# A two-layer decoder trunk in fp32: the lower part of every fourth weight chunk is formed on GpSimd instead of VectorE

## The chip, the cores and the metric

The kernel runs on one core of a Trainium2 chip. The metric is device time in microseconds (us) of one execution, as the median of a few runs. A profiler recorded one execution; its times are used for everything below that is finer than the whole run. Five engines work side by side and meet through semaphores: TensorE (PE, its weight loads shown as PEld), VectorE (DVE), ScalarE (ACT), GpSimd (POOL) and SyncE (SP, which here issues nearly all DMAs).

## What is computed

Two layers, each on 256 rows of width 2048. In short (`S`, `sigmoid` and `rms` as usual, everything fp32):

```python
h = rms_norm(x, norm_g[l])
proj = h @ w_in[l]                      # 2048 x 18496, split into the parts of four branches
y_pool = pool_mixer(pv, pool_w, pool_scale) * silu(pz)      # causal means over 2, 4, 8, 16 rows
y_mla  = mla_mixer(cq, ckv, kr, ...) * silu(mz)             # 8-head latent attention with rotary part
y_conv = conv_mixer(cb, cc, cx, conv_w) * silu(cz)          # gated convolution of width 3
y_mem  = memory_xattn(xq, rms_norm(mem) @ w_mem_kv, ...) * silu(xz)
merged = sum(sigmoid(gpre[i] + gate_b[i]) * (y[i] @ w_branch[l, i]) for i in range(4))
x = x + merged @ w_out[l]
```

Nearly all arithmetic is in the products with the weights, which are read once each: 478 MB in all.

## The kernel before

**A product in three terms.** TensorE multiplies operands in a reduced-precision fp32 form (type fp32r). To get close to fp32, every operand is kept as two fp32r tiles: `hi`, the value rounded by a copy into that type, and `lo`, what is left, `value - hi`. A product is then hi·hi + hi·lo + lo·hi. The activations' pairs are made once and kept; the weights' pairs are made as the weights arrive.

**Chunks.** The weights lie packed in HBM in the order of use, in chunks of 128 partitions by up to 1024 elements (512 KB); there are 884 of them in the two layers. The generator `wchunks` (L293) handles a chunk in three steps: L303 loads it into `raw` (issued by SP), L304 rounds it into `hi` on ACT, L305 subtracts, `lo = raw - hi`, on DVE. All three stand under `tc.high_priority(AHEAD)`, with AHEAD = 100, so that the framework's scheduler places them ahead of other work that comes earlier in the program. There are four `raw` buffers, three `hi` and three `lo`, used in turn: the chunk that comes three later can write its `hi` only after TensorE has finished with the present one.

**Consumers.** `tm_block` (L308 on) uses a chunk as the moving operand: per chunk twelve matmuls of 128x512, in threes L317 (activation hi, weight hi), L318 (activation hi, weight lo) and L319 (activation lo, weight hi). `fm_block` uses it as the stationary operand: per chunk eight pairs L323 (weight hi, 512 columns) and L324 (weight lo, 256 columns). Every block accumulates in one of three PSUM tiles `acc`; the layer's other work (transposes at L350, L401, L459 and others, attention, norms, gates) runs beside the blocks, with its TensorE parts between the blocks' matmuls.

**What sets the order.** A scheduler of the framework orders each engine's instructions at build time, by its own estimate of when each would be ready; an engine then works strictly in that order. POOL holds almost nothing before: some constants and twelve small fills, of `pv` at L738 and of `u` at L783.

**The start.** The first four blocks (chunks 1 to 32) are the keys and values of the memory. Beside them the kernel takes the statistics of x: four row loads at L386, each followed by two squares with a sum on ACT (L197, `junk`), then a chain of small DVE operations (L376, then L185 to L191) that ends in `rx` (L377). Two transposes at L401 spread `rx` over the partitions, and the operands of `h` are made from it.

Of the kernel before, what the change touches and what calls it, by code (L numbers as in the profile page):

```python
# [10 lines left out]
F32 = mybir.dt.float32  # L11
# [3 lines left out]
ALU = mybir.AluOpType  # L15
# [95 lines left out]
def tile_hybrid_trunk(  # L111
    ctx: ExitStack, tc: tile.TileContext, x, xT, mem, memT, positions, vectors, mla_g, gate_b, weights, consts, out,
):
    nc = tc.nc
    V, A, T = nc.vector, nc.scalar, nc.tensor
# [12 lines left out]
    def nm(s):  # L128
        uid[0] += 1
        return f"{s}{uid[0]}"  # L130
# [147 lines left out]
    def step():  # L278
        if background:
            run = background.pop(0)  # L280
            if run is not None:
                run()
# [5 lines left out]
    def defer(runs, delay):  # L288
        if len(background) < delay:
            background.extend([None] * (delay - len(background)))  # L290
        background.extend(runs)

    def wchunks(l, name, c0):  # L293
        off, n, nk, kt = plan[name, c0]
        m = nk * n
        for k0 in range(0, kt, nk):
            raw = wp.tile([P, 1024], F32, tag="raw", name=nm("raw"), bufs=4)
            hi = wp.tile([P, 1024], F32R, tag="hi", name=nm("hi"), bufs=3)
            lo = wp.tile([P, 1024], F32R, tag="lo", name=nm("lo"), bufs=3)
            o = off + P * n * k0  # L300
            step()
            with tc.high_priority(AHEAD):
                nc.sync.dma_start(raw[:, :m], weights[l, o : o + P * m].rearrange("(p m) -> p m", p=P))  # L303
                A.copy(hi[:, :m], raw[:, :m])  # L304
                V.tensor_tensor(lo[:, :m], raw[:, :m], hi[:, :m].bitcast(F32), ALU.subtract)  # L305
            yield k0, nk, kt, n, *(w[:, :m].rearrange("p (k n) -> p k n", n=n) for w in (hi, lo))

    def tm_block(lhs, l, name, c0):  # L308
        ps = acc()
        for k0, nk, kt, n, hi, lo in wchunks(l, name, c0):  # L310
            for k in range(nk):
                kk = k0 + k
                o = lhs(kk // 2) if callable(lhs) else lhs[kk // 2]
                for t in range(2):
                    hh = o[:, kk % 2, 0, t * P : (t + 1) * P]
                    hl = o[:, kk % 2, 1, t * P : (t + 1) * P]
                    T.matmul(ps[:, t, :n], hh, hi[:, k, :], start=kk == 0, stop=False)  # L317
                    T.matmul(ps[:, t, :n], hh, lo[:, k, :], start=False, stop=False)  # L318
                    T.matmul(ps[:, t, :n], hl, hi[:, k, :], start=False, stop=kk == kt - 1)  # L319
        return ps  # L320
# [5 lines left out]
    def fm_block(rhs, l, name, c0):  # L326
        ps = acc()
        for k0, nk, kt, n, hi, lo in wchunks(l, name, c0):
            for j in range(2):
                for k in range(nk):  # L330
                    kk = k0 + k
                    fm_tile(ps, j, hi, lo, rhs[kk // 2], kk % 2, k, j * P, kk == 0, kk == kt - 1)
        return ps
# [396 lines left out]
    def pool_branch(l, vec, h):  # L730
# [24 lines left out]
        for b in range(2):  # L755
            sz = silu_block(h, l, OFF["pz"] + 512 * b)
            (_, _, _, _, hi, lo), = wchunks(l, "pool", 512 * b)
            for i in range(2):
                g = 2 * b + i
                ps = acc()  # L760
                for j in range(2):
                    for k in range(2):
                        fm_tile(ps, j, hi, lo, mixed[g], k, 2 * i + k, j * P, k == 0, k == 1)
                y = t2("yp").rearrange("p (n s) -> p n s", n=2)
                fm_sum(y, ps)
                for j in range(2):
                    V.scalar_tensor_tensor(
                        y[:, j, :], y[:, j, :], gcol(vec, "pool_scale", 2 * g + j), sz[:, 2 * i + j, :], ALU.mult, ALU.mult
                    )
                o = opnd()  # L770
                split(o, y)
                ys.append(o)
# [211 lines left out]
```

## Time and profile before

| what | value |
|---|---|
| median of three runs | 2520.2 us (2517.4, 2520.2, 2521.82) |
| profiled execution, first to last instruction (span) | 2517.2 us |
| busy: PE / PEld / DVE / ACT / POOL | 2503.9 / 2108.3 / 1539.0 / 1248.4 / 1.6 us |
| chain of work that ended last | PE 97%, DVE 1%, ACT 1% |
| granted TensorE clock, mean | 1.000 (full, 2.4 GHz) |

The profile gives the profiled execution's own time as its span; the median of the runs is 3.0 us above that span. The chain of work is followed back from the last instruction, at each step to what released it; an engine that is busy 61% of the time but has 1% of the chain is nearly always ahead of need. A row of the timeline reads: start in us, length in us, engine, line, operation, what it writes and reads, and in brackets how long the engine stood idle before it and what ended that.

### The profile page before, as it was taken

How to read it: one execution, taken by the hardware profiler on the slowest of the kernel's cores; microseconds unless marked ns; L12 is line 12 of the kernel's file. 1: busy time of each engine (PE TensorE's matmuls, PEld its weight loads, DVE VectorE, ACT ScalarE, POOL GpSimd, SP SyncE). 2: the span in 40 equal slices, each digit the busy share in tenths (PEclk: the TensorE clock that was granted, in tenths of full speed). 3: DMA queues.
4: the chain of work that ended last, by engine and by line, in shares of the span. 5: the costliest groups of instructions: out<-in, count | busy, mean ns of one | idle time of the engine just before them, and what ended most of it. 6: DMA issues, size and time to landing. Idle time of an engine off the chain costs nothing.

```text
span 2517.2 us, 32451 instructions
## 1 busy us (share of the span) xinstructions
PE 2503.9 (99%) x12402; PEld 2108.3 (84%) x12402; DVE 1539.0 (61%) x2132; ACT 1248.4 (50%) x1707; POOL 1.6 (0%) x16
## 2 busy tenths in 40 slices
PE   8999999999999999999999999999999999999999
PEld 7888888888888888888888888888888888888887
DVE  6767775566556655556474577755765565555554
ACT  7556674445444444445454566744444444444443
POOL 0000000000000000000000000000000000000000
PEclk9999999999999999999999999999999999999999
DMA  8665436655655566667655654366556655566565
GB/s 314 207 198 162 145 128 197 202 188 192 201 196 186 188 221 203 201 195 231 220 187 167 202 166 136 128 202 204 186 191 202 194 187 188 193 202 203 189 229 164
DMA packets 143676, 484.22 MB, mean 192 GB/s; under 512 B 16160, under 2 KB 17184, under 8 KB 143520
## 3 DMA queue, kind: packets, MB, share of 16 engines
q1 hardware_dynamic: 142800, 481.06, 58.5%
q8 instruction: 97, 1.59, 0.3%
q10 hardware_dynamic: 720, 1.09, 0.1%
q14 instruction: 59, 0.48, 0.1%
HBM read 477.89 MB, written 4.19 MB: 192 GB/s over the span
## 4 chain that ended last, share of the span: by engine, by line
PE 97%; DVE 1%; ACT 1%; DMA 0%; issue 0%; DVEq 0%; SPq 0%; ACTq 0%
PE acc L319 22%; PE acc L318 22%; PE acc L317 22%; PE acc L323 19%; PE acc L324 10%; PE ms L703 1%; PE ms L702 1%; PE ms L350 1%; DVE lo L305 0%; ACT junk L197 0%; PE ms L551 0%; PE ms L552 0%; PE ms L553 0%; DMA row<-in_x_dram 0%; ACT hi L304 0%; PE ms L722 0%
## 5 line engine op out<-in xcount | busy, mean ns | idle before, releaser
L305 DVE TENSOR_TENSOR lo<-raw,hi 128x1024 fp32r<-128x1024 f32 (+2 forms) x884 | 1062.4, 1202 | 869.8 <-ACT hi L304 867.0
L304 ACT CAST hi<-raw 128x1024 fp32r<-128x1024 f32 (+2 forms) x884 | 914.7, 1035 | 1179.1 <-PE acc L319 791.2
L317 PE MATMUL acc<-hi,op 128*128 128x512 f32 (+2 forms) x2496 | 962.5, 386 | 5.8 <-ACT op L392 5.7
L318 PE MATMUL acc<-lo,op 128*128 128x512 f32 (+2 forms) x2496 | 957.9, 384 | 1.7 <-DVE lo L305 1.7
L319 PE MATMUL acc<-hi,op 128*128 128x512 f32 (+2 forms) x2496 | 958.1, 384 | 0.0
L323 PE MATMUL acc<-op,hi 128*128 128x512 f32 x2080 | 736.9, 398 | 0.1
L324 PE MATMUL acc<-op,lo 128*128 128x256 f32 x2080 | 585.7, 282 | 0.0
L317 PEld LDWEIGHTS acc<-hi,op 128*128 128x128 f32 x2496 | 469.2, 188 | 95.2 <-ACT op L392 6.2
L319 PEld LDWEIGHTS acc<-hi,op 128*128 128x128 f32 x2496 | 469.0, 188 | 92.0 <-issue 1.3
L318 PEld LDWEIGHTS acc<-lo,op 128*128 128x128 f32 x2496 | 469.4, 188 | 91.1 <-DVE lo L305 2.9
L323 PEld LDWEIGHTS acc<-op,hi 128*128 128x128 f32 x2080 | 390.8, 188 | 94.3 <-DVE z L338 0.8
L324 PEld LDWEIGHTS acc<-op,lo 128*128 128x128 f32 x2080 | 392.9, 189 | 1.9 <-issue 1.3
L814 DVE TENSOR_TENSOR g<-acc,gb 128x1024 f32<-128x1024 f32 x32 | 39.2, 1224 | 12.7 <-PE acc L319 12.7
L337 ACT COPY fmt<-acc 128x512 f32<-128x512 f32 x72 | 41.4, 581 | 0.0
L815 ACT ACTIVATE g<-g 128x1024 f32<-128x1024 f32 x32 | 34.0, 1062 | 6.7 <-DVE g L814 6.7
L821 DVE TENSOR_TENSOR g<-g,acc 128x1024 f32<-128x1024 f32 x24 | 29.3, 1221 | 9.8 <-PE acc L319 9.8
L822 DVE TENSOR_TENSOR merged<-merged,g 128x1024 f32<-128x1024 f32 x24 | 29.2, 1219 | 0.0
L513 ACT ACTIVATE sm<-sm,smx,rqs 128x128 f32<-128x128 f32 (+1 forms) x32 | 17.3, 540 | 22.3 <-DVE smx L511 22.3
L494 DVE TENSOR_TENSOR z<-z,sg 128x512 f32<-128x512 f32 x32 | 22.0, 688 | 7.8 <-ACT sg L493 7.7
L197 ACT ACTIVATE junk<-acc 128x256 f32<-128x256 f32 (+2 forms) x68 | 25.2, 371 | 2.1 <-PE acc L319 1.2
L392 ACT ACTIVATE op<-ms,gt 128x256 fp32r<-128x256 f32 x32 | 15.1, 471 | 14.0 <-DVE op L393 14.0
L338 DVE TENSOR_TENSOR z<-acc,fmt 128x512 f32<-128x512 f32 x32 | 21.9, 684 | 0.0
(193 smaller groups left out, 949.1 us busy)
## 6 DMA issues: line engine op xcount, KB each, us to landing
raw<-in_weights_dram SPq DMA_DIRECT2D x836, 512.0 KB, 3.5
raw<-in_weights_dram SPq DMA_DIRECT2D x32, 288.0 KB, 2.8
gb<-in_gate_b_dram SPq DMA_DIRECT2D x32, 256.0 KB, 4.4
raw<-in_weights_dram SPq DMA_DIRECT2D x16, 384.0 KB, 3.1
mt<-in_memT_dram SPq DMA_DIRECT2D x14, 256.0 KB, 5.7
row<-in_mem_dram SPq DMA_DIRECT2D x4, 512.0 KB, 8.4
row<-in_x_dram SPq DMA_DIRECT2D x4, 512.0 KB, 8.2
xt<-in_xT_dram SPq DMA_DIRECT2D x8, 256.0 KB, 5.5
```

Of the source, the lines that this page charges most:

```text
L304: A.copy(hi[:, :m], raw[:, :m])
L305: V.tensor_tensor(lo[:, :m], raw[:, :m], hi[:, :m].bitcast(F32), ALU.subtract)
L317: T.matmul(ps[:, t, :n], hh, hi[:, k, :], start=kk == 0, stop=False)
L318: T.matmul(ps[:, t, :n], hh, lo[:, k, :], start=False, stop=False)
L319: T.matmul(ps[:, t, :n], hl, hi[:, k, :], start=False, stop=kk == kt - 1)
L323: T.matmul(ps[:, j, :], hi[:, k, n0 : n0 + P], o[:, half].rearrange("p a s -> p (a s)"), start=first, stop=False)
L324: T.matmul(ps[:, j, :S], lo[:, k, n0 : n0 + P], o[:, half, 0, :], start=False, stop=last)
L337: A.copy(tmp, ps[:, :, S:])
L814: V.tensor_tensor(g, pg, gb.unsqueeze(1).broadcast_to([P, 2, 512]), ALU.add)
L815: A.activation(g, g, AF.Sigmoid)
L821: V.tensor_tensor(g, g, pb, ALU.mult)
L822: V.tensor_tensor(mg, mg, g, ALU.add)
```

## The change

A counter numbers the chunks from 1. A chunk whose number is divisible by four has its `lo` computed by GpSimd, by the same operation on the same tiles; the other three of four stay on VectorE. Loads, roundings and matmuls are as before.

```diff
@@ -290,6 +290,8 @@
             background.extend([None] * (delay - len(background)))
         background.extend(runs)
 
+    nchunk = [0]
+
     def wchunks(l, name, c0):
         off, n, nk, kt = plan[name, c0]
         m = nk * n
@@ -302,7 +304,9 @@
             with tc.high_priority(AHEAD):
                 nc.sync.dma_start(raw[:, :m], weights[l, o : o + P * m].rearrange("(p m) -> p m", p=P))
                 A.copy(hi[:, :m], raw[:, :m])
-                V.tensor_tensor(lo[:, :m], raw[:, :m], hi[:, :m].bitcast(F32), ALU.subtract)
+                nchunk[0] += 1
+                eng = nc.gpsimd if nchunk[0] % 4 == 0 else V
+                eng.tensor_tensor(lo[:, :m], raw[:, :m], hi[:, :m].bitcast(F32), ALU.subtract)
             yield k0, nk, kt, n, *(w[:, :m].rearrange("p (k n) -> p k n", n=n) for w in (hi, lo))
```

In the changed kernel the lines after it stand two to four lower: the load is L305, the rounding L306, the subtraction L309, the three matmuls L321 to L323, the fills L742 and L787, the row loads L390, the transposes of `rx` L405.

Since the scheduler works by its own estimate, other instructions move too. The first place is the start, where the squares of x's rows meet the roundings. On ACT (`hi_558` belongs to chunk 16, `hi_617` to chunk 17, `junk_372` to `junk_446` are the eight squares of the four row loads) the order before is:

```order
L304 CAST hi_558<-raw_557 128x1024
L197 ACTIVATE junk_372,ssp_87<-row_370 128x512
L197 ACTIVATE junk_374,ssp_87<-row_370 128x512
L197 ACTIVATE junk_396,ssp_87<-row_394 128x512
L304 CAST hi_617<-raw_616 128x1024
L197 ACTIVATE junk_398,ssp_87<-row_394 128x512
L197 ACTIVATE junk_420,ssp_87<-row_418 128x512
L197 ACTIVATE junk_422,ssp_87<-row_418 128x512
L197 ACTIVATE junk_444,ssp_87<-row_442 128x512
L197 ACTIVATE junk_446,ssp_87<-row_442 128x512
```

and with the change, on the same engine:

```order
L197 ACTIVATE junk_372,ssp_88<-row_370 128x512
L197 ACTIVATE junk_374,ssp_88<-row_370 128x512
L306 CAST hi_558<-raw_557 128x1024
L197 ACTIVATE junk_396,ssp_88<-row_394 128x512
L197 ACTIVATE junk_398,ssp_88<-row_394 128x512
L197 ACTIVATE junk_420,ssp_88<-row_418 128x512
L197 ACTIVATE junk_422,ssp_88<-row_418 128x512
L197 ACTIVATE junk_444,ssp_88<-row_442 128x512
L197 ACTIVATE junk_446,ssp_88<-row_442 128x512
L306 CAST hi_617<-raw_616 128x1024
```

The rounding of chunk 16 now stands behind two squares, that of chunk 17 behind all eight. SP's queue at the same place, before:

```order
L303 DMA raw_557<-in_weights_dram 128x1024
L303 DMA raw_616<-in_weights_dram 128x1024
L386 DMA row_370<-in_x_dram 128x2x512
L386 DMA row_394<-in_x_dram 128x2x512
L386 DMA row_418<-in_x_dram 128x2x512
L386 DMA row_442<-in_x_dram 128x2x512
L159 DMA gt_500<-in_vectors_dram 128x76
```

and with the change:

```order
L305 DMA raw_557<-in_weights_dram 128x1024
L390 DMA row_370<-in_x_dram 128x2x512
L390 DMA row_394<-in_x_dram 128x2x512
L390 DMA row_418<-in_x_dram 128x2x512
L390 DMA row_442<-in_x_dram 128x2x512
L305 DMA raw_616<-in_weights_dram 128x1024
L159 DMA gt_500<-in_vectors_dram 128x76
```

The load of chunk 17 went from ahead of the four row loads to behind them. The second place is on PE, a little later: the two transposes of `rx` among the matmuls of chunks 17 (`lo_618`) and 18 (`lo_644`). Before:

```order
L318 MATMUL acc_615<-lo_618,op_99 128x512
L319 MATMUL acc_615<-hi_617,op_99 128x512
L317 MATMUL acc_615<-hi_643,op_125 128x512
L318 MATMUL acc_615<-lo_644,op_125 128x512
L401 MATMUL ms_538<-cst,rx 128x128 x2
L319 MATMUL acc_615<-hi_643,op_125 128x512
```

and with the change:

```order
L323 MATMUL acc_366<-hi_558,op_316 128x512
L321 MATMUL acc_615<-hi_617,op_99 128x512
L322 MATMUL acc_615<-lo_618,op_99 128x512
L323 MATMUL acc_615<-hi_617,op_99 128x512
L321 MATMUL acc_615<-hi_617,op_99 128x512
L405 MATMUL ms_538<-cst,rx 128x128 x2
L322 MATMUL acc_615<-lo_618,op_99 128x512
```

The transposes moved forward past ten matmuls: they stood behind two of chunk 18, and stand now behind four of chunk 17. The third place is POOL's queue around one of the fills of the pooling branch; before, nothing but fills stands there:

```order
L738 MEMSET pv_4876 128x2x16
L738 MEMSET pv_4979 128x2x16
L738 MEMSET pv_5084 128x2x16
L783 MEMSET u_6653 128x4x2
L783 MEMSET u_7424 128x4x2
```

and with the change (`lo_5064` is chunk 184, `lo_5172` chunk 188):

```order
L742 MEMSET pv_4979 128x2x16
L309 TENSOR_TENSOR lo_4959<-raw_4957,hi_4958 128x1024
L309 TENSOR_TENSOR lo_5064<-raw_5062,hi_5063 128x1024
L742 MEMSET pv_5084 128x2x16
L309 TENSOR_TENSOR lo_5172<-raw_5170,hi_5171 128x1024
L309 TENSOR_TENSOR lo_5267<-raw_5265,hi_5266 128x1024
```

The fills now share a queue with 221 subtractions and stand between them.

## Rows read from the trace of the kernel before

**Rows 1.** The page: span, busy time by engine, the chain that ended last.
```profile
span 2517.2 us, 32451 instructions
PE 2503.9 (99%) x12402; PEld 2108.3 (84%) x12402; DVE 1539.0 (61%) x2132; ACT 1248.4 (50%) x1707; POOL 1.6 (0%) x16
...
PE 97%; DVE 1%; ACT 1%; DMA 0%; issue 0%; DVEq 0%; SPq 0%; ACTq 0%
```
**Rows 2.** Waits of PE: engine line, awaited: us in total, times, longest.
```profile
PE acc L317 <- ACT op L392: 5.7, 1, 5.7
PE acc L318 <- DVE lo L305: 1.7, 1, 1.7
```
**Rows 3.** Groups by shape: busy us, mean ns of one, idle before and releasers.
```profile
L305 DVE TENSOR_TENSOR lo<-raw,hi 128x1024 fp32r<-128x1024 f32 x836 | 1022.9, 1224 | 834.7 <-ACT hi L304 832.1 <-PE acc L324 1.7
...
L304 ACT CAST hi<-raw 128x1024 fp32r<-128x1024 f32 x836 | 879.8, 1053 | 1133.6 <-PE acc L319 759.6 <-PE acc L323 295.6 <-issue 45.0
```
**Rows 4.** Timeline of a quiet stretch: two roundings, a subtraction, a weight load.
```profile
1207.89 1.05 ACT L304 CAST hi<-raw 128x1024 fp32r<-128x1024 f32 x1 [1.67 <-PE acc L319]
...
1208.98 1.22 DVE L305 TENSOR_TENSOR lo<-raw,hi 128x1024 fp32r<-128x1024 f32 x1 [1.50 <-ACT hi L304]
...
1210.61 1.05 ACT L304 CAST hi<-raw 128x1024 fp32r<-128x1024 f32 x1 [1.67 <-PE acc L319]
...
1213.13 0.19 PEld L318 LDWEIGHTS acc<-lo,op 128*128 128x128 f32 x1
```
**Rows 5.** Groups by shape on POOL.
```profile
L738 POOL MEMSET pv<- 128x32 f32 x8 | 1.0, 125 | 1606.7 <-DVE op L342 1305.9 <-DVE merged L819 179.9 <-DVE ps L745 116.5
L783 POOL MEMSET u<- 128x8 f32 x4 | 0.4, 106 | 341.7 <-DVE merged L822 241.2 <-DVE yp L767 100.5
```
**Rows 6.** Timeline of ACT at the start, chunks 12, 16 and 17 and squares.
```profile
34.45 1.04 ACT L304 CAST hi<-raw 128x1024 fp32r<-128x1024 f32 x1
...
44.67 1.05 ACT L304 CAST hi<-raw 128x1024 fp32r<-128x1024 f32 x1 [1.66 <-PE acc L319]
46.83 0.63 ACT L197 ACTIVATE junk<-row 128x512 f32<-128x512 f32 x1 [1.11 <-DMA row<-in_x_dram]
...
47.59 0.63 ACT L197 ACTIVATE junk<-row 128x512 f32<-128x512 f32 x1
...
48.97 1.04 ACT L304 CAST hi<-raw 128x1024 fp32r<-128x1024 f32 x1
```
**Rows 7.** The chain at the start: start, us, what.
```profile
38.31 1.23 DVE lo L305
39.94 6.87 DMA row<-in_x_dram
```
**Rows 8.** Timeline of PE at the start.
```profile
50.13 0.39 PE L318 MATMUL acc<-lo,op 128*128 128x512 f32 x1
...
57.40 0.49 PE L318 MATMUL acc<-lo,op 128*128 128x512 f32 x1 [1.65 <-DVE lo L305]
57.74 0.43 PE L401 MATMUL ms<-cst,rx 128*128 128x128 f32 x2
57.93 0.48 PE L319 MATMUL acc<-hi,op 128*128 128x512 f32 x1
```
**Rows 9.** Timeline of DVE at the start: first and last of the chain to `rx`.
```profile
53.69 0.16 DVE L376 TENSOR_REDUCE ss<-ssp 128x2 f32<-128x8 f32 x1 [0.86 <-ACT junk L197]
...
57.52 0.16 DVE L377 COPY rx<-rs 128x2 f32<-128x2 f32 x1
```
**Rows 10.** Busy time in a stretch: all engines; then DVE at L305 alone.
```profile
500.00:600.00 100.00, 99.83 (x562) 86.06 (x561) 68.56 (x82) 48.68 (x58) 0.23 (x2) 1.00 0.57 187
...
500.00:600.00 100.00, 42.87 (x36) 1.00 0.57 187
```
**Rows 11.** Timeline: the fill of `pv_5084` on POOL, and the subtraction of chunk 188.
```profile
526.81 0.12 POOL L738 MEMSET pv<- 128x32 f32 x1 [58.26 <-DVE ps L745]
...
549.27 1.22 DVE L305 TENSOR_TENSOR lo<-raw,hi 128x1024 fp32r<-128x1024 f32 x1
```

## The prediction

> **What bounds the kernel now.** I read the page's first lines first: TensorE is busy for 2503.9 of 2517.2 us and the chain that ended last is 97% TensorE, while VectorE, busy for 61%, has 1% of the chain [rows 1]. So VectorE's work is taken off an engine that is not the bound, and the question is only whether TensorE ever waits for a `lo` tile, before and after. The list of waits says how much there is to win: TensorE waited once for 5.7 us, before its very first matmul, which waits for ACT, and once for 1.7 us for a `lo` [rows 2]. The second is all that a relief of VectorE can give back.
>
> Next the timeline of a quiet stretch, for the slack of one chunk. Roundings start every 2.72 us (1207.89, 1210.61), each released by TensorE's end of the chunk three before. The rounding that starts at 1207.89 ends at 1208.94, the subtraction runs from 1208.98 to 1210.20, and TensorE loads the first weights with that `lo` at 1213.13 [rows 4]. (That it is this one follows from three buffers: two chunks of 2.72 us lie between the release and the use.) From the end of the rounding to the use there are 4.19 us; VectorE takes 1.22 of them, and 2.93 are left over. A subtraction on another engine may thus take three times as long and nobody waits.
>
> **What is removed.** 221 of 884 subtractions leave VectorE, nearly all at 1.22 us [rows 3]: 221 x 1.22 = 270 us, and its busy time falls from 1539 to about 1270 us. On the path this is worth between nothing and 1.7 us.
>
> **What is added.** 221 subtractions on GpSimd. The trace of before has no such operation there. The nearest rows of the same engine are two fills: 32 elements per partition in 125 ns, 8 in 106 ns [rows 5], hence 0.79 ns per element written and 0.10 us fixed. From below: if a subtraction went at the pace of a fill, 1024 elements would take 0.91 us. From above: a subtraction moves three streams, two read and one written; one after the other they take 3 x 0.81 + 0.10 = 2.53 us. VectorE's own 1.22 us lies between. I take 2.53, because the work is three streams and a fill is one. At 2.53 the subtraction of a quiet chunk ends 4.19 - 2.53 = 1.66 us before its use, at 0.91 it ends 3.28 us before: both ends cost nothing there. The Trainium skill (GPSIMD Engine Reference, section "Elementwise — side-by-side cycle accounting") has 4497 ns for a two-input add of 2048 elements, so by halves an estimate of 2.25 us here; by it the sum would come out the same.
>
> The chunk after a GpSimd chunk has its rounding done 2.72 us later, when 2.53 us of subtraction are over; in quiet stretches the two engines do not even run at the same time. The `raw` buffer of a GpSimd chunk comes free 1.3 us later than before; the rounding that next needs it comes four chunks, 10.9 us, after the present one, so the load has ample time.
>
> **What moves.** The scheduler placed other instructions anew. Where TensorE's order alone changes by some matmuls, in the attention part, a matmul is only exchanged with another; I cost that at nothing, between -1 and +2 us for both layers together, under cover of the same full queue of matmuls. The start is another matter, since there the chain of waits did leave TensorE. Step by step, for chunks 16 to 18:
>
> - The rounding of chunk 12 ended at 35.49 [rows 6]; GpSimd takes it to 38.05. SP's load of chunk 16 waits for that buffer, and the four loads of x's rows now stand right behind it. Before, they stood behind the load of chunk 17 too, which waited for the subtraction of chunk 13 (38.31 + 1.23 = 39.54), and were issued from 39.94 on, with 6.87 us to the first square [rows 7]. Now: about 38.5 + 6.9 = 45.4.
> - ACT does two squares of 0.76 us each (46.83 to 47.59, [rows 6]) ahead of chunk 16's rounding, which starts at 46.9 instead of 44.67. It ends at 48.0, GpSimd at 50.5; TensorE wanted it at 50.13 [rows 8]. Late by 0.4 us (not late at 0.91 us per subtraction).
> - Six more squares come ahead of chunk 17's rounding: 48.0 + 6 x 0.76 = 52.5, instead of 48.97. It ends at 53.6, its `lo` near 55. TensorE is there at about 53.
> - The squares are done at 52.5, about 1.2 us sooner than before (the sum over them started at 53.69). From there to the copy into `rx` were 3.83 us, one `lo` of 1.2 us among them [rows 9], and one stands among them now. So `rx` is copied near 56.4 to 56.8 instead of 57.52.
> - TensorE's transposes of `rx` now stand in chunk 17 after four matmuls. They can run near 56.8. Behind them are 8 matmuls of chunk 17 and 12 of chunk 18, at 2.72/12 = 0.227 us: chunk 18 ends near 56.8 + 0.2 + 20 x 0.227 = 61.5. Before, TensorE waited for chunk 18's `lo` until 57.40 and after the transposes went on at 57.93 with 10 matmuls [rows 8], so to 60.2.
>
> So about 1.3 us are lost at the start, between 0.5 (everything a little sooner) and 3 (`rx` later, another late chunk after it).
>
> **Sum.** Relief 0 to -1.7, of which I count nothing, since the place where it would show is the one that is reordered; start +1.3; attention parts 0; a few late chunks elsewhere +0.5. That gives 2517.2 + 1.8 = 2519.0 for the span, and with the 3.0 us by which the median of the runs lies above that span 2522. Without surprises the range of this case is 2518 to 2525. A measurement of this kernel can tell about 0.2%, here 5 us, from no change.
>
> **Rival 1, slower: the two engines hinder one another.** Both read two SBUF tiles per subtraction. If they exclude each other, the point from which it matters is the second VectorE operation in front of GpSimd's: 2.53 + 1.22 = 3.75 is within 4.19, 2.53 + 2 x 1.22 = 4.97 is 0.78 too late. Outside the quiet stretches VectorE does 68.56 - 42.87 = 25.7 us of other work in 100 [rows 10]. If two such operations stand in front by chance, one chunk in 15 (0.257 squared), that is 221 x 0.066 x 0.78 = 11 us, or 2533; clumps, as in softmax and convolution, could make it 2540. For it: the busy stretches and two inputs on both sides. Against it: not every stretch is as busy, much of VectorE's other work has one operand in PSUM, and VectorE has 2.9 us of slack when it is the one held up. The Trainium skill (SBUF — State Buffer, section "Who interferes with whom") states that a VectorE instruction with two SBUF inputs contends with a GpSimd instruction that reads SBUF and that the loser is blocked for the whole instruction; no row of before shows both engines at work. Chance 0.23.
>
> **Rival 2, much slower: one subtraction takes over 4.19 us.** Then all quiet chunks are late; at 5 us it would be 221 x 0.8 = 179 us, about 2700. Against it is only the estimate by rows of fills. Chance 0.04.
>
> **Rival 3, the fills of POOL hold up subtractions.** POOL works in order, and a fill waits for a free tile; a subtraction behind it would wait too. At `pv_5084` the tile was free at 526.81, and the fill now stands behind the subtraction of chunk 184, ahead of chunk 188's, done at 549.27 before [rows 11]: 20 us to spare. The other eleven stand likewise, later than they ran. One late fill would cost some us and give about 2526. Chance 0.01.
>
> **Rival 4, faster.** The 1.7 us come back and the start does not lose: 2518 to 2519. It is measured as no change. To fall over 5 us below, luck of the runs (they spread over 4.4 us) would have to be added: chance 0.06.
>
> That the change does not do what it says can be excluded: POOL's order holds 221 subtractions.
>
> **How the numbers follow.** Forecast 2522, chance 0.66, all of it counted as no change. Slower by over 0.2%: rivals 1 to 3, 0.28. Faster: 0.06. The range goes from 2516, the lower edge with the spread of the runs, to 2538, which takes in most of rival 1.
>
> **What would show it.** POOL at L309 with 221 instructions of 2.2 to 2.6 us, busy for about 540 us; VectorE near 1270 us; TensorE's share of the chain still 97%, with waits for `lo` under 5 us in all; at the start a pause of some us in chunk 17, before the transposes of `rx`, in place of that in chunk 18. Rival 1 would show as VectorE's subtractions well over 1.22 us in the mean, GpSimd's near 3 us or more, and many short waits of TensorE for POOL. The prediction is wrong if such waits sum to over 5 us, or if the matmuls themselves, which I leave at 0.227 us, change their pace.

## The result and the profile after

The changed kernel takes 2529.03 us in the median of five runs (2527.98 to 2531.99), before 2520.2 us: a ratio of 1.0039 over the runs, 95% interval [1.0027, 1.0051] (the two medians alone give 1.0035). It is slower by 8.8 us. That lies within the range that was given, but on the side of rival 1 (2533 us), not of the likeliest case (2522 us, no change). The profiled execution has a span of 2527.2 us, 10.0 above that of before.

The page after has the lines that answer to [rows 1], and the groups by shape those to [rows 3]:

```profile
span 2527.2 us, 32532 instructions
PE 2506.4 (99%) x12402; PEld 2107.9 (83%) x12402; DVE 1363.5 (54%) x1911; ACT 1248.4 (49%) x1707; POOL 525.6 (21%) x237
...
PE 95%; DVE 3%; ACT 1%; issue 1%; DMA 0%; POOL 0%; DVEq 0%; SPq 0%; ACTq 0%
```

```profile
L309 DVE TENSOR_TENSOR lo<-raw,hi 128x1024 fp32r<-128x1024 f32 x627 | 770.5, 1229 | 873.6 <-ACT hi L306 872.9 <-issue 0.2
...
L309 POOL TENSOR_TENSOR lo<-raw,hi 128x1024 fp32r<-128x1024 f32 x209 | 506.0, 2421 | 1908.4 <-ACT hi L306 1870.3 <-DVE rs L186 10.7 <-DVE posf L203 9.9
...
L498 DVE TENSOR_TENSOR z<-z,sg 128x512 f32<-128x512 f32 x32 | 34.2, 1070 | 16.5 <-ACT sg L497 16.3
L397 DVE SCALAR_TENSOR_TENSOR op<-mt,gt,op 128x256 fp32r<-128x256 f32 x32 | 19.6, 652 | 3.1 <-ACT op L396 3.1
```

The subtractions themselves look as forecast: 221 on POOL (by all shapes), 2.42 us in the mean at full size, and VectorE's own still at 1.23. The surprise is VectorE's total. It should fall from 1539.0 by 221 times about 1.2 us, to some 1275; it is 1363.5, so nearly 90 us came in elsewhere. The last two rows show where: the same 32 instructions took 688 and 478 ns before:

```profile
L494 DVE TENSOR_TENSOR z<-z,sg 128x512 f32<-128x512 f32 x32 | 22.0, 688 | 7.8 <-ACT sg L493 7.7
...
L393 DVE SCALAR_TENSOR_TENSOR op<-mt,gt,op 128x256 fp32r<-128x256 f32 x32 | 13.9, 478 | 0.0
```

Set against the usual length of their line and shape, 51 VectorE instructions of the changed kernel are more than 0.2 us too long, 85 us in sum; before, none is. The plainest one stands in the timeline of DVE and POOL at 60 us:

```profile
59.83 0.17 DVE L186 TENSOR_SCALAR rs<-rs 128x4 int32<-128x4 int32 x1
60.00 2.40 POOL L309 TENSOR_TENSOR lo<-raw,hi 128x1024 fp32r<-128x1024 f32 x1 [10.71 <-DVE rs L186]
60.02 2.40 DVE L187 TENSOR_SCALAR rs<-rs 128x4 int32<-128x4 int32 x1
62.46 0.16 DVE L189 SCALAR_TENSOR_TENSOR rs<-rs 128x4 f32<-128x4 f32 x1
```

An operation on four elements per partition, 0.17 us long in the row above it, lasts 2.40 us, from just after GpSimd's start to GpSimd's end. It is not slowed, it is held. And all that stands behind it on VectorE waits too. Which instructions are held depends on where their operands lie: 58 VectorE instructions with an operand in PSUM (`acc`, `ms`) began while a GpSimd subtraction had over 0.4 us to go, and all 58 kept their usual length; none of the 51 held ones has such an operand.

What TensorE waits for now (engine line, awaited: us in total, times, longest; compare [rows 2]):

```profile
PE acc L321 <- ACT op L396: 5.8, 1, 5.8
PE ms L556 <- DVE op L346: 3.2, 3, 1.7
PE ms L684 <- DVE yf L729: 1.9, 1, 1.9
PE acc L322 <- DVE lo L309: 1.7, 3, 1.1
PE acc L322 <- POOL lo L309: 1.0, 1, 1.0
PE ms L405 <- DVE rx L381: 0.6, 1, 0.6
PE acc L328 <- DVE lo L309: 0.5, 1, 0.5
PE ms L689 <- DVE yf L729: 0.4, 1, 0.4
```

Nearly all new waits are for VectorE; one of 1.0 us is for GpSimd. One of the longest, 1.70 us, seen in the timeline of POOL, DVE and PE:

```profile
359.10 2.39 POOL L309 TENSOR_TENSOR lo<-raw,hi 128x1024 fp32r<-128x1024 f32 x1 [15.89 <-ACT hi L306]
359.52 2.52 DVE L346 TENSOR_TENSOR op<-xq,op 128x512 fp32r<-128x512 f32 x1 [0.66 <-ACT op L345]
361.96 0.68 DVE L346 TENSOR_TENSOR op<-kvm,op 128x512 fp32r<-128x512 f32 x1
...
362.70 0.38 PE L556 MATMUL ms<-op,op 128*128 128x256 f32 x1 [1.70 <-DVE op L346]
```

The lower half of an operand of the memory's attention takes 2.52 us instead of 0.68, its neighbour comes behind it, and the scores' matmul stands still for 1.70 us.

By place (start of each chunk's first matmul in both traces): +3.5 us up to chunk 32, +1.4 from there to chunk 100, +3.5 from there to chunk 130, +1.8 near chunk 550, and about nothing over the rest. From chunk 130 to 530, 1094 us of the span, the shift stays between 8.3 and 8.9 us although 100 subtractions run on GpSimd there.

### The profile page after: what moved, and what is told of

The parts are those of the page before. It is cut to its first block, busy times and chain, and to the rows that moved or that the text cites. A ratio compares the mean times of both kernels' runs of the same rounds, so it can differ in the third digit from the quotient of the medians.

```text
span 2527.2 us, 32532 instructions
## 1 busy us (share of the span) xinstructions
PE 2506.4 (99%) x12402; PEld 2107.9 (83%) x12402; DVE 1363.5 (54%) x1911; ACT 1248.4 (49%) x1707; POOL 525.6 (21%) x237
## 3 DMA queue, kind: packets, MB, share of 16 engines
HBM read 477.89 MB, written 4.19 MB: 191 GB/s over the span
## 4 chain that ended last, share of the span: by engine, by line
PE 95%; DVE 3%; ACT 1%; issue 1%; DMA 0%; POOL 0%; DVEq 0%; SPq 0%; ACTq 0%
PE acc L323 21%; PE acc L322 21%; PE acc L321 21%; PE acc L327 19%; PE acc L328 9%; DVE lo L309 1%; PE ms L707 1%; PE ms L706 1%; PE ms L354 1%; ACT hi L306 0%; ACT junk L197 0%; PE ms L556 0%; PE ms L726 0%; DVE op L397 0%; PE ms L557 0%
## 5 line engine op out<-in xcount | busy, mean ns | idle before, releaser
L306 ACT CAST hi<-raw 128x1024 fp32r<-128x1024 f32 (+2 forms) x884 | 913.9, 1034 | 1157.5 <-PE acc L323 776.4
L309 DVE TENSOR_TENSOR lo<-raw,hi 128x1024 fp32r<-128x1024 f32 (+2 forms) x663 | 801.1, 1209 | 912.1 <-ACT hi L306 911.2
L321 PE MATMUL acc<-hi,op 128*128 128x512 f32 (+2 forms) x2496 | 962.6, 386 | 5.9 <-ACT op L396 5.8
L323 PE MATMUL acc<-hi,op 128*128 128x512 f32 (+2 forms) x2496 | 958.1, 384 | 0.0
L309 POOL TENSOR_TENSOR lo<-raw,hi 128x1024 fp32r<-128x1024 f32 (+2 forms) x221 | 524.8, 2374 | 1991.4 <-ACT hi L306 1945.5
L321 PEld LDWEIGHTS acc<-hi,op 128*128 128x128 f32 x2496 | 469.1, 188 | 94.8 <-ACT op L396 6.3
L323 PEld LDWEIGHTS acc<-hi,op 128*128 128x128 f32 x2496 | 468.9, 188 | 91.9 <-issue 1.0
L498 DVE TENSOR_TENSOR z<-z,sg 128x512 f32<-128x512 f32 x32 | 34.2, 1070 | 16.5 <-ACT sg L497 16.3
```

The costliest lines, as they stand in the source:

```text
L309: eng.tensor_tensor(lo[:, :m], raw[:, :m], hi[:, :m].bitcast(F32), ALU.subtract)
L498: V.tensor_tensor(z[:, sl, :], z[:, sl, :], sg, ALU.mult)
```

## Experiments

Theory A: a GpSimd subtraction holds any VectorE instruction of certain kinds until it ends, and the time is lost where TensorE soon needs what stands behind. Theory B: the new order of the instructions costs the time. In all kernels below the order on every engine is pinned, either to that of before or to that of after, so that only what is named differs. The diffs show the line that is changed in short; the code that pins the order is left out. "Held" is counted as above. Each is compared with runs of the kernel before on the same chip (2519.25 to 2520.33 us).

**The assignment without the new order.** Order of before; `nchunk[0] % 4 == 0` on GpSimd as in the change.

> Every fourth subtraction on GpSimd, but every engine's instructions pinned to the order of the kernel before (GpSimd's in the place that they had there). Theory A (the two engines block one another: in the changed kernel's trace 51 VectorE instructions last over 0.2 us longer than usual, 85 us in sum, the longest by about 2.2 us, one GpSimd subtraction): 2525 to 2531 us, with VectorE's busy time again some 60 to 100 us above the 1277 us that its own work takes. Theory B (the scheduler's new order costs the time): 2519 to 2522 us, as before. If both count, between, 2522 to 2525.

2526.94 us, ratio 1.0027 [1.0017, 1.0037]: +6.6 us, as theory A has it. 49 instructions held, 84.0 us. TensorE's wait for `yf`, 0.5 us before, is now:

```profile
PE ms L685 <- DVE yf L730: 3.7, 2, 2.3
```

By place in this trace: +3.3 us up to chunk 32, +3.1 from chunk 100 to 130, +1.2 near 550. Part of the 3.3 us is a lower clock. Behind two pauses of 0.72 and 1.75 us, at 56.5 and 58.7 us, the granted clock of TensorE fell to the lower of its two levels, 1.2 GHz, and eight matmuls took 0.43 us each instead of 0.23, 1.6 us in all; before, behind one pause of 1.65 us, it stayed at 2.4 GHz. The same four microseconds in this kernel and then in the kernel before (busy us and instructions of PE, PEld, DVE, ACT, POOL; granted clock; DMA):

```profile
59.00:63.00 4.00, 4.00 (x13) 3.15 (x13) 3.93 (x7) 1.05 (x1) 2.71 (x1) 0.57 0.79 260
```

```profile
59.00:63.00 4.00, 4.00 (x19) 3.33 (x18) 3.90 (x10) 2.09 (x4) 0.00 (x0) 1.00 0.88 313
```

**The new order without the assignment.**

```diff
-                eng = nc.gpsimd if nchunk[0] % 4 == 0 else V
+                eng = V        # order on every engine as with the line above
```

> All subtractions on VectorE as before, but every engine's instructions pinned to the order of the changed kernel (the moved subtractions in the place that they have there on GpSimd). Theory A (blocking): 2518 to 2522 us, no loss. Theory B (order): 2526 to 2531 us. The step of the prediction on the start (reordering costs 0.5 to 3 us there) would show here as 2521 to 2523 us.

2523.59 us, ratio 1.0014 [1.0005, 1.0023]: +3.3 us; none held. At chunk 32 the shift is 0.04 us, so the start in its new order costs nothing by itself that can be told (a trace below, whose start is that of before, is at -1.2 there); it is 1.0 at chunk 110 and 2.4 at chunk 130, so most of this loss lies in the attention. There TensorE waits for short steps of VectorE:

```profile
PE ms L557 <- DVE op L347: 1.3, 2, 0.9
...
PE ms L690 <- DVE yf L730: 0.9, 1, 0.9
```

Both theories hold a part: 6.6 + 3.3 = 9.9, observed 8.8.

**GpSimd only writes.** Order of after.

```diff
-                eng.tensor_tensor(lo[:, :m], raw[:, :m], hi[:, :m].bitcast(F32), ALU.subtract)
+                nc.gpsimd.memset(lo[:, :m].bitcast(F32), 0.0)      # every fourth chunk
```

> Order of the changed kernel, but GpSimd fills every fourth lo with zeros instead of subtracting: it only writes, and reads nothing from SBUF. The lower part of every fourth weight chunk is left out of the result. By the rows of small fills one should take about 0.9 us. Theory A: holds are shorter and only some VectorE instructions are held at all, the ones with two SBUF inputs (z at L498, 1070 ns in the mean with the change, 688 before) run at their usual pace; blocked time in sum under 25 us; 2518 to 2524 us. Theory B (order): 2526 to 2531 us, as the order is the same.

2517.39 us, ratio 0.999 [0.9981, 0.9999], just below theory A's range. The fills read nothing and take 0.96 us; 10 VectorE instructions are held for 4.3 us in sum, all TENSOR_SCALAR:

```profile
L311 POOL MEMSET lo<- 128x1024 f32 x209 | 199.8, 956 | 2197.8 <-PE acc L326 1382.2 <-PE acc L332 374.5 <-DVE op L350 84.3
```

It is 6.2 us faster than the same order with everything on VectorE, so a relief of VectorE is worth something where the order makes VectorE late. (A fill also starts without waiting for the rounding, so this is an upper bound on what a free helper would give.)

**Twice as many.** Order of before, `nchunk[0] % 2 == 0`.

> Every second subtraction on GpSimd (442), pinned to the order of the kernel before. Theory A: twice the holds and fewer VectorE instructions that can dodge them: 2535 to 2560 us. Theory B: 2519 to 2523 us, since the order is the old one. A third reading, that GpSimd's longer subtraction alone is late where slack is short (2.40 us against 1.22): about twice what e1 loses, and the waits of TensorE would name GpSimd, not VectorE.

2554.89 us, ratio 1.014 [1.0123, 1.0158]: +34.6 us, five times the loss for twice the subtractions, within theory A's range. 114 held, 190 us, set against their length in the kernel before, and TensorE now waits in many places, for VectorE more than for GpSimd:

```profile
PE acc L323 <- DVE lo L310: 7.8, 5, 3.1
...
PE ms L685 <- DVE yf L730: 5.7, 2, 2.9
PE acc L323 <- POOL lo L310: 3.0, 2, 1.9
PE ms L406 <- DVE rx L382: 2.8, 1, 2.8
```

Not all of the 34.6 us is waiting: in the profiled execution the granted clock was 0.62 in the mean from 63 to 72 us and 0.79 from 322 to 330.

**By place.** Order of before. One kernel has every fourth subtraction on GpSimd only in the long blocks of projections and outputs (159), the next only in the rest (62).

```diff
-                eng = nc.gpsimd if nchunk[0] % 4 == 0 else V
+                n = nchunk[0]
+                eng = nc.gpsimd if n % 4 == 0 and (124 < n <= 441 or n > 565) else V
```

> Only chunks 125 to 441 and 566 to 884, which lie in the long blocks of projections and outputs, have every fourth subtraction on GpSimd (159 of the 221); every engine's order is that of before. In the kernel with all 221 on GpSimd in the order of before (2526.9 us) these chunks held 17 VectorE instructions for 33 us in sum, and the work of TensorE shifted by only +0.1 us over the first stretch and -0.4 over the second. Theory A (only a hold in front of something that TensorE will soon need is paid, and that is in the memory's and the attention's parts): VectorE still held some 15 to 20 times for about 35 us, POOL busy for about 378 us, and no loss: 2519.5 to 2521.5 us. Rival (each subtraction on GpSimd costs its share wherever it stands, by pressure on SBUF or by small waits that add up): 159/221 of 6.6 us, so about +4.7, 2525 us.

2518.8 us, ratio 0.9997 [0.9988, 1.0006], with 17 held for 33.5 us. So pinning the order costs nothing by itself either.

> The complement: only in chunks 1 to 124 and 442 to 565 is every fourth subtraction on GpSimd (62 of the 221), order of before. Theory A: nearly the whole loss of the kernel with 221: 2525.5 to 2527.5 us, with some 30 VectorE instructions held for about 50 us and the waits of TensorE for yf and lo as there. Rival (a share for each subtraction): 62/221 of 6.6, +1.9, so 2522 us.

2526.49 us, ratio 1.0028 [1.0017, 1.004]: the whole loss, with 62 subtractions and 32 held for 50.7 us. The start is that of the kernel with all 221; here the clock stays at 1.00, and the shift at chunk 32 is 1.8 us. A share for each subtraction is ruled out. The page of the first and its waits show 159 subtractions at the same price, and no one who waits for them:

```profile
PE 2503.4 (99%) x12402; PEld 2107.9 (84%) x12402; DVE 1379.0 (55%) x1973; ACT 1249.0 (50%) x1707; POOL 383.9 (15%) x175
```

```profile
PE acc L322 <- ACT op L397: 6.0, 1, 6.0
PE acc L323 <- DVE lo L310: 0.8, 1, 0.8
PE ms L685 <- DVE yf L730: 0.5, 2, 0.2
```

**Two halves.** Order of before; each GpSimd subtraction as two of 512 columns.

```diff
-                eng.tensor_tensor(lo[:, :m], raw[:, :m], hi[:, :m].bitcast(F32), ALU.subtract)
+                for part in (slice(0, m // 2), slice(m // 2, m)):      # every fourth chunk
+                    nc.gpsimd.tensor_tensor(lo[:, part], raw[:, part], hi[:, part].bitcast(F32), ALU.subtract)
```

> Every fourth subtraction on GpSimd, but as two instructions of half the width (128x512), order of before. Each should take 1.2 to 1.3 us, so POOL stays busy for about 530 to 560 us. Theory A (a GpSimd instruction has the access for its whole length, and whoever comes meanwhile waits to its end): a VectorE instruction now waits 1.25 us at most and goes in between the halves, so the VectorE time in holds falls from 84 us to about half, and the loss of 6.6 us to 1.5 to 3.5: 2522 to 2524 us. Now GpSimd's second half may be the one that waits: some halves of 2 us and more. Rival (what counts is GpSimd's time in sum, or the two engines slow each other in proportion): the loss stays at 6 to 7 us, 2526 to 2528.

2526.93 us, ratio 1.0028 [1.0017, 1.0039]: +7.7 us. The forecast of half the loss failed, and so did that of half the time in holds: 82 are held for 73.1 us. The rival's number came true, but not its ground: 159 subtractions cost nothing above, so GpSimd's time in sum is not what counts. The reason is seen at chunk 108. With one piece (order of before), DVE, POOL and PE:

```profile
303.48 2.37 POOL L310 TENSOR_TENSOR lo<-raw,hi 128x1024 fp32r<-128x1024 f32 x1 [10.99 <-ACT hi L307]
...
303.64 2.35 DVE L274 TENSOR_TENSOR rr<-rp 128x128 f32<-128x128 f32 x1
305.92 0.28 DVE L275 TENSOR_TENSOR rr<-rp 128x128 f32<-128x128 f32 x1
306.12 0.74 DVE L730 TENSOR_TENSOR yf<-ms,z 128x256 f32<-128x256 f32 x2
...
306.58 0.66 PE L685 MATMUL ms<-cst,qg 128*128 128x128 f32 x4 [2.25 <-DVE yf L730]
```

and with two:

```profile
301.76 2.56 POOL L313 TENSOR_TENSOR lo<-raw,hi 128x512 fp32r<-128x512 f32 x2 [10.85 <-ACT hi L307]
...
301.92 1.27 DVE L274 TENSOR_TENSOR rr<-rp 128x128 f32<-128x128 f32 x1
303.11 1.35 DVE L275 TENSOR_TENSOR rr<-rp 128x128 f32<-128x128 f32 x1
304.38 0.74 DVE L735 TENSOR_TENSOR yf<-ms,z 128x256 f32<-128x256 f32 x2
...
304.85 1.11 PE L690 MATMUL ms<-cst,qg 128*128 128x128 f32 x4 [2.24 <-DVE yf L735]
```

Between the halves one VectorE instruction of 0.28 us gets through, and the next is held by the second half. In a run of short VectorE instructions two holds of 1 us come to the same as one of 2, and TensorE waits 2.24 instead of 2.25 us. (The four matmuls behind the wait take 1.11 us instead of 0.66, as the granted clock fell here:

```profile
304.00:309.00 5.00, 4.15 (x20) 3.77 (x21) 3.01 (x7) 2.43 (x5) 0.31 (x1) 0.66 0.33 108
```

with one piece it fell at the start instead.) No gain is shown at the start: the shift at chunk 32 is 1.6 us, against 1.8 in the kernel with 62 whole subtractions, where the clock was full too.

**One input instead of two.** Order of before; in every fourth chunk GpSimd copies `raw` into `lo`.

```diff
-                eng.tensor_tensor(lo[:, :m], raw[:, :m], hi[:, :m].bitcast(F32), ALU.subtract)
+                nc.gpsimd.tensor_copy(lo[:, :m], raw[:, :m])      # every fourth chunk
```

> In every fourth chunk GpSimd only copies raw into lo (one tile read instead of two; the subtraction of hi is left out), order of before. From rows seen: a fill of this size takes 0.93 us, the subtraction 2.40; a copy between them, 1.2 to 1.8 us. Theory A with any read of SBUF on GpSimd's side being enough to hold: VectorE's subtractions and other instructions with two inputs in SBUF are held as before, each for at most the copy's length; 25 to 45 held, 25 to 50 us in sum, and the loss is 1.5 to 4 us: 2522 to 2524.5. Rival (it takes two inputs on both sides): no TENSOR_TENSOR of VectorE is held, only a few TENSOR_SCALAR as beside the fills, and the time is 2517.5 to 2520.5.

2518.75 us, ratio 0.9996 [0.9987, 1.0006]: no loss, against theory A's number, but the holds are there as it said: 41 for 31.5 us, 22 of them TENSOR_TENSOR. So one input read by GpSimd is enough to hold, and two on both sides are not needed. The holds are at most as long as a copy, which takes less than half of a subtraction (1.04 us as a rule; the mean below has 40 copies of up to 1.87 us in it, which VectorE held up in turn):

```profile
L311 POOL CAST lo<-raw 128x1024 fp32r<-128x1024 f32 x209 | 236.5, 1131 | 2161.6 <-PE acc L326 1351.4 <-PE acc L332 355.0 <-DVE op L350 95.6
```

Whether the loss went because holds are shorter or because a copy, which doesn't wait for the rounding, falls on other instructions, this run does not tell.

**Five chunks given back.** Order of before; 216 of the 221 on GpSimd.

```diff
-                eng = nc.gpsimd if nchunk[0] % 4 == 0 else V
+                n = nchunk[0]
+                eng = nc.gpsimd if n % 4 == 0 and n not in (12, 24, 108, 120, 548) else V
```

> Every fourth subtraction on GpSimd in the order of before, except in five chunks (12, 24, 108, 120, 548), which stay on VectorE: 216 of the 221 remain. In the trace with all 221 each of these five held a VectorE instruction shortly ahead of a pause of TensorE (55.4 and 56.5 us: 2.9 us; 79.9: 0.4; 303.9: 2.4; 363.3: 1.0; 1559.1: 1.6). Theory A (a hold costs only where TensorE waits for what stands behind the held instruction): VectorE is still held some 40 times for about 75 us, the waits for yf, rx and op at these places go, and the loss falls from 6.6 us to between 0 and 2: 2519.5 to 2522 us; a neighbouring hold may take the place of one. Rival (a share for each subtraction, or for each hold): 216/221 of the loss stays, 2525.5 to 2527 us.

2521.09 us, ratio 1.0005 [0.9996, 1.0014]. Of +6.6 us (2526.94 against 2520.33) +1.4 is left (2521.09 against 2519.69), though 44 VectorE instructions are still held, for 74 us. Of the waits for `yf`, 3.7 us with all 221, this is left:

```profile
PE ms L685 <- DVE yf L730: 0.4, 2, 0.3
```

So, by the medians, about 5 us of the loss hang on five holds of 49. The traces show 4.3 us of it at the three in attention: from chunk 100 to 560 the shift grows by 4.4 us with all 221, by 0.1 here. For chunks 12 and 24 they show no gain: the shift at chunk 32 is 3.3 us in both. The profiled execution took 2523.09 us, 2.0 above the median; its first row of x needed 7.74 us instead of 6.92, and its clock fell as in the other (0.66 in the mean from 59 to 64 us). What the two at the start cost thus stays open.

## Why the prediction was right and wrong

The range held; the likeliest case, no change, did not. The sum gave a span of 2519.0 us, 1.8 above before; it is 2527.2, 10.0 above. (The 3.0 us between span and median were those of before; after, they are 1.8.)

**Right: the price on GpSimd.** 2.53 was taken, 2.42 is the mean, and 2.40 the usual one. But the way to it was luck. By 0.81 us for each stream a copy, with two, should take 1.72 us; it takes 1.04, and a fill 0.96. The second input alone adds 1.36 us. The estimate by the Trainium skill's figure (GPSIMD Engine Reference, "Elementwise — side-by-side cycle accounting"), 2.25, was low by 0.17.

**Right: the slack of a quiet chunk.** The subtraction of a quiet chunk ends 1.65 us before its use, forecast 1.66. Its rounding starts at 1210.93 and the use is 5.24 us behind that, as in [rows 4]:

```profile
1212.12 2.40 POOL L309 TENSOR_TENSOR lo<-raw,hi 128x1024 fp32r<-128x1024 f32 x1 [8.47 <-ACT hi L306]
...
1216.17 0.19 PEld L322 LDWEIGHTS acc<-lo,op 128*128 128x128 f32 x1
```

The quiet blocks cost nothing, as forecast and as the kernel with 159 confirms. Rivals 2 and 3 fell with this: the usual price is far from 4.19 us, and no wait points to a fill.

**Wrong: the start, +1.3 us by reordering.** The term was right in place, too small, and wrong in cause. The new order alone moves the start by 0.04 us: `rx` is copied at 54.85 in the changed kernel, not at 56.4 to 56.8, which may pay for the roundings that stand behind squares. In the order of before the start is 1.8 and 3.3 us later with the holds (the 3.3 with 1.6 us of low clock), with both changes 3.5. One of the holds is chunk 12's, here in the order of before: it holds a scaling of the keys' statistics (35.82, +2.16 us), the subtraction of chunk 13 comes 1.26 us later than in [rows 7], and with it the load of chunk 17 and the row loads in SP's queue, the very chain that the prediction followed for another reason.

**Wrong: the attention parts, 0 (-1 to +2).** The step "a matmul is only exchanged with another" asked only about PE. The order alone costs 3.3 us, nearly all there and later, and the holds add more. What TensorE waits for in attention are VectorE's short steps (`op`, `yf`), which came just in time before. The list of waits of before has a third row that says so, and the prediction, which read two, left it out:

```profile
PE ms L680 <- DVE yf L725: 0.5, 2, 0.2
```

**Wrong: what a few late chunks cost elsewhere, +0.5, and rival 1's victim.** Rival 1 had the mechanism, mutual exclusion, and the sign. Its price was worked out for a GpSimd that comes late behind two VectorE instructions (11 us). The trace shows the other side held: GpSimd's subtraction exceeds 2.45 us in 8 of 221 cases, VectorE is held in 51. The prediction dismissed that with "VectorE has 2.9 us of slack when it is the one held up". That slack is the subtraction's. The instructions of the start and of attention have less: `yf` was 0.23 us late in before already, so a hold of 2.06 us became a wait of 2.25:

```profile
300.68 0.66 PE L680 MATMUL ms<-cst,qg 128*128 128x128 f32 x4 [0.23 <-DVE yf L725]
```

The rule that was cited there (the Trainium skill, SBUF — State Buffer, "Who interferes with whom": a VectorE instruction with two SBUF inputs contends with a GpSimd instruction that reads SBUF, and the loser is blocked for all of it) agrees with every run here for instructions with two inputs: held beside subtraction and copy, not beside the fill. It should have had more than 0.23.

The signs that were set for rival 1 would have missed it, too: VectorE's subtractions stayed at 1.23 us and GpSimd's at 2.42, and TensorE's waits for POOL sum to 1.0 us. What shows it is VectorE's total, 1363.5 us where 1270 was forecast, and TensorE's share of the chain, 95% where 97% was.

**The relief, counted 0.** In the order of before it is not worth more than that: with 159 subtractions off VectorE where nothing is lost, the ratio is 0.9997. In the order of after a relief without reads is worth up to 6.2 us; the subtractions' holds eat it up.

Open is why the two parts, 6.6 and 3.3 us, give 8.8 and not 9.9; each is known only to about 2.5 us. It was also not tried which other phase than every fourth from the fourth would meet fewer of the short steps.

## What to carry to other kernels

When work is moved to GpSimd that reads SBUF, don't ask only whether GpSimd is in time. Ask which VectorE instructions will run meanwhile, and what slack each of these has: a hold costs nothing in front of work with 2.9 us of slack and its full length in front of a step that TensorE takes at once; a pause of TensorE can cost some more behind it, by the clock (1.6 us here). If it is done at all, choose the chunks by what VectorE does beside them, and don't expect shorter pieces to help where VectorE has a run of short instructions.

## What the runs showed of the hardware beyond what was expected

A TENSOR_SCALAR on 128x4 integers, with one tensor input, is held like the others (2.40 us instead of 0.17), and beside GpSimd's fills, which read nothing, TENSOR_SCALAR is the only kind that is held (10 times, 4.3 us). GpSimd's price does not grow evenly with the number of streams: 0.96 us for a fill of 128x1024, 1.04 for a copy, 2.40 for a subtraction that nothing holds; two half subtractions take 2.56 together.
